# A mixture of experts on one core: the rows beyond 128 of a large expert in fp32 on four column tiles, and one chain of expert pairs

## The chip, the cores and the metric

The kernel runs on one core of a Trainium2 chip. The metric is the device time of one execution in microseconds. The core has TensorE (PE, with its weight loads shown apart as PEld), VectorE (DVE), ScalarE (ACT), GpSimd (POOL) and SyncE (SP), which issues most transfers. Engines run side by side and wait for each other through semaphores.

## The reference, cut to what matters

Two transformer blocks run one after the other on 512 rows of width 1024. The second one ends in a mixture of 32 experts, each row going to 4 of them:

```python
logits = (xf @ w_router + b_router).astype(jnp.float32)
top_v, top_i = lax.top_k(logits, TOP_K)
w = jax.nn.softmax(top_v, axis=-1)
...
h = lax.ragged_dot(xs, w_up, sizes) + b_up[sorted_e]
g, lin = jnp.split(h, 2, axis=-1)
g = jnp.minimum(g, SWIGLU_LIMIT)
lin = jnp.clip(lin, -SWIGLU_LIMIT, SWIGLU_LIMIT)
act = g * jax.nn.sigmoid(SWIGLU_ALPHA * g) * (lin + 1.0)
y = lax.ragged_dot(act, w_down, sizes) + b_down[sorted_e]
y = y * w.reshape(-1)[order][:, None].astype(y.dtype)
return jax.ops.segment_sum(y, tok, num_segments=n).reshape(B, T, D)
```

An expert has 1024 by 2048 and 1024 by 1024 fp32 weights, 12 MiB. Which rows it gets, and how many, is known only when the kernel runs.

## The kernel before, in words

The program is written out in order; a framework adds the semaphores. Everything up to the router is not touched by the change. In the experts' part (`moe`, from L1140) each expert's weights come as 12 chunks of 1 MiB, 8 for the up matrix and 4 for the down matrix, into a ring of 8 buffers of 128x2048. SP issues a chunk's transfer (`fetch`, L1120 in the trace) once the buffer's old content has been used (`refill`, L1131).

There are three ways to compute an expert:

- **`expert(e, two)`** (L1424), up to 128 rows. Each chunk is split into a high and a low fp32r part (`split`, L214: ACT copies, DVE subtracts), two chunks ahead, and its buffer is refilled right after. A step (`part`, L1323) is 4 k by 3 matmuls of 512 columns: x high by w high, x high by w low, x low by w high.
- **`few(e)`** (L1511), up to 64 rows, in fp32 straight from the ring (`halves`, L1488): two column tiles of 64 side by side, each a half of the columns, 8 matmuls of 256 columns a step. The buffer is refilled after its matmuls.
- **the second tile**, rows 128 to 191 of an expert, inside `expert` when `two` is 64 (`second`, L1444). It uses the split weights, two steps behind the first tile. Its 64 rows stand beside their low parts, so that a step is 8 matmuls of 512 columns and `sums` (L1438) adds the halves of the result.

The numbers of rows per expert are sorted on the chip (`order`, L1725), and `places` (L1208) branches on them: expert 0 first, in the form that its count asks for (`kind`); then, if any expert has still more rows, a loop (`far`) that loads its weights once more; then the pairs of a large expert (odd numbers) and a small one (even numbers). `seconds` (L1235) is a nest of up to 6 pairs with a second tile, left when t0, the number of experts with over 128 rows, is reached. Six single branches and `pairs` (L1241) take the other large ones, up to nP pairs; `rest` takes the small ones in between and `few(31)` is last.

What one expert prepares for the next stands in `ahead` (L1549): the row numbers of four experts at a time (`slots`, in step 6 of every expert with e % 4 == 1), the gather of the rows of expert e + 2 on POOL's queue in step 2, and their transposes (`flip`, L1311), which share two PSUM buffers (`tr`) with `slots`. `further` (L1564) does the same for the second tile. `finish` (L1366) weights an expert's result and scatters it with an add into the output rows on POOL's queue; a large expert's result is finished in step 0 of the small one that follows. The result tile `y` is also where `few` keeps its activations for the down matrix (`hf`, copied at L1541).

The order of the second tile and the first in `expert`:

```python
for i in range(12):
    n = e * 12 + i
    if two and i > 1:
        second(i - 2)
    if i < 10 or not e:
        self.unfold(n + 2)
    if i < 2:
        self.refill(n)
    self.part(self.bank(e, i), x if i < 8 else m["h"], i, self.pairs[n % self.PAIRS], one)
```

Of the kernel before, what the change touches and what calls it, by code (L numbers as in the profile page):

```python
# [11 lines left out]
F32 = mybir.dt.float32  # L12
# [22 lines left out]
def constants():  # L35
    c = np.zeros((128, CSTW), np.float32)

    def put(name, a):
# [25 lines left out]
                                e > 0, 128 + 64 * (e == 0) + 128 * (p[:, None] // 32), e, np.zeros((128, 7))], 1))  # L64
# [23 lines left out]
def lay_out(inp):  # L88
# [27 lines left out]
    for j in range(4):  # L116
# [19 lines left out]
        a["w_up_2"][0][..., q.ravel()].reshape(NE, 2, 4, 128, 4, 512).transpose(0, 4, 1, 3, 2, 5)).reshape(NE, 8, 128, 2048)  # L136
    o["w_dn2"] = np.ascontiguousarray(
        a["w_down_2"][0].reshape(NE, 2, 4, 128, 2, 512).transpose(0, 4, 1, 3, 2, 5)).reshape(NE, 4, 128, 2048)
# [17 lines left out]
class K:  # L156
# [983 lines left out]
    def moe(self):  # L1140
        tc, nc, a = self.tc, self.nc, self.a
        with ExitStack() as es:
# [26 lines left out]
            m["one64"] = mp.tile([128, 2, 128], F32R, name="one64")  # L1169
            nc.vector.memset(m["one64"].bitcast(F32), 0.0)  # L1170
# [35 lines left out]
    SECOND = 6  # L1206

    def places(self, srt):  # L1208
# [6 lines left out]
        kind = load(0, 2)  # L1215
        with tc.If(kind > 0) as cmp:
            with tc.If(kind < 2) as cm2:
                self.expert(0, 0)
            with cm2.Else():
                self.expert(0, 64)  # L1220
        with cmp.Else():
            self.few(0)
        nfar, nP, t0 = load(7, 64), load(1, 15), load(2, self.SECOND)
        with tc.If(nfar > 0):
            self.extra(srt)
            with tc.For_i(0, nfar, 1) as it:
                er = nc.values_load(self.li[0:1, ds(it, 1)], engines=(mybir.EngineType.SP, mybir.EngineType.DVE),
                                    min_val=0, max_val=NE - 1, skip_runtime_bounds_check_because="an expert's number")
                self.far(er, it)
# [5 lines left out]
        def seconds(t):  # L1235
            if t < self.SECOND:
                with tc.If(t0 > t):
                    pair(t, 64)
                    seconds(t + 1)
# [18 lines left out]
        seconds(0)  # L1258
        for lo in range(0, self.SECOND, 3):
            with tc.If(t0 < lo + 3):  # L1260
                for t in range(lo, lo + 3):
                    with tc.If(t0 < t + 1):
                        with tc.If(nP > t):
                            pair(t, 0)
        pairs(self.SECOND)
# [73 lines left out]
    def swiglu(self, i, bank, act, rows=128):  # L1339

        nc, m = self.nc, self.m
        j = i // 2
        if i not in (3, 5, 7):
            return
        n = 512 if j == 1 else 256
        pg, pl = (bank(0), bank(2)) if j == 1 else (bank(i - 1)[:, :256], bank(i - 1)[:, 256:])
        self.gated(pg, pl, act[:rows, 512 * (j > 1) + 256 * (j > 2):][:, :n])

    def gated(self, pg, pl, act):
        nc, m = self.nc, self.m  # L1350
        rows, n = act.shape
        sg = m["sg"][:rows, :n]
        nc.scalar.activation(sg, pg, AF.Relu, scale=-1.0, bias=m["seven"][:rows, 0:1])  # L1353
# [70 lines left out]
    def expert(self, e, two):  # L1424
        nc, m = self.nc, self.m
        one = m["one"][e % 2]
        x = m["x"][e % 2]
        sb = m["sl"][2]
        bb = m["bb"]
        self.numbers(e)  # L1430
        if two and not e:
            self.further(e)
        if two == 64:
            nc.vector.tensor_copy(m["one64"][:, :, :64], one[:, :, :64])
        xt = m["xb"][0]
        xb, tmp = ((xt[:, :, :64], xt[:, :, 64:]), m["y"][0][:64]) if two == 64 else (m["xb"], None)

        def sums(p, to):  # L1438

            nc.scalar.activation(to, p[64:], AF.Copy)  # L1440
            nc.vector.tensor_tensor(to, to, p[:64], op=OP.add)
            return to

        def second(i):  # L1444
            if i == 8:
                self.flip(m["actb"][0], xb, n=two)
            bank = lambda i: bb[i // 2 % 2] if i < 8 else bb[i % 2]
            self.part(bank(i), xt if two == 64 else xb, i, self.pairs[(e * 12 + i) % self.PAIRS],
                      m["one64"] if two == 64 else one, two)
            if two == 64 and i in (3, 5, 7):  # L1450
                h = [sums(bank(j), tmp[:, 512 * (j // 2 % 2):][:, :512]) for j in ((0, 2) if i == 3 else (i,))]
                self.swiglu(i, lambda j: h[min(j // 2, len(h) - 1)], m["actb"][0], 64)
            elif two == 128:
                self.swiglu(i, bank, m["actb"][0])

        for i in range(12):
            n = e * 12 + i
            if two and i > 1:
                second(i - 2)
            if i < 10 or not e:  # L1460
                self.unfold(n + 2)
            if i < 2:
# [466 lines left out]
```

## Time and profile before

| | us |
|---|---|
| median of 3 runs (2643.07 to 2645.09) | 2645.02 |
| time of the profiled execution | 2647.34 |
| its span | 2645.5 |
| busy in the span: PE | 2437.4 (92%) |
| PEld | 1948.2 (74%) |
| DVE | 1345.4 (51%) |
| ACT | 1062.9 (40%) |
| POOL | 191.7 (7%) |

The span is from the first to the last instruction; the time of an execution also has what lies around it. The experts' first matmul with weights (L1330) starts at 1335.9 us. Before that the two blocks' attention and dense layers run, and behind the experts a short tail. PE's busy time counts matmuls that overlap in the pipeline, so that a stretch with a busy PE need not run at its highest rate; the starts of instructions tell more. The mean granted TensorE clock is 0.966 of the full 2.4 GHz. A large expert can be told in the timeline by its first bias matmul (L1330, 512 columns), a small one by L1505 and L1509 (256 columns), and a second tile by its PSUM tile `pv`.

### The profile page before, as it was taken

The numbers are of one execution on the slowest core, as the hardware profiler recorded it, in microseconds if no ns is written. First come the engines' busy times: TensorE is split into PE (matmuls) and PEld (weight loads), VectorE is DVE, ScalarE is ACT, GpSimd is POOL, SyncE is SP. The second block draws the span as 40 slices with busy tenths as digits, with TensorE's granted clock in tenths as the row PEclk, the third lists the DMA queues.
The fourth block names the chain that finished last, engine by engine and source line by source line (L and its number), as shares of the span: only waits on it lengthen the run. The fifth ranks groups of instructions, "written<-read, shape, count | busy, mean of one in ns | idle before, by whom it ended". The sixth has DMA issues, their size and how long they took to land. (4 is left out here: it accounts for less than half of the span.)

```text
span 2645.5 us, 39434 instructions
## 1 busy us (share of the span) xinstructions
PE 2437.4 (92%) x15686; PEld 1948.2 (74%) x15686; DVE 1345.4 (51%) x2493; ACT 1062.9 (40%) x1596; POOL 191.7 (7%) x183
## 2 busy tenths in 40 slices
PE   7999999999999999999879899799999999688888
PEld 5799978898899899889857667476666666444457
DVE  6766753344333444467576536465656565121135
ACT  5755552223322325566354434344444444111123
POOL 0021100000000000000010100111100111000000
PEclk9999999999999999999989999899999999899999
DMA  4122222322222311210585966899999999899991
GB/s 157 64 94 71 77 72 96 124 92 80 96 96 87 121 54 65 83 60 2 186 291 195 350 248 237 303 374 366 404 376 402 366 402 377 297 400 399 400 380 41
DMA packets 86919, 554.54 MB, mean 210 GB/s; under 512 B 11783, under 2 KB 12935, under 8 KB 25368
## 3 DMA queue, kind: packets, MB, share of 16 engines
q1 hardware_dynamic: 71280, 508.33, 49.3%
q0 software_dynamic: 8784, 31.59, 4.7%
q10 hardware_dynamic: 6616, 11.53, 1.3%
q8 instruction: 138, 2.26, 0.4%
q14 instruction: 101, 0.83, 0.1%
HBM read 531.60 MB, written 19.81 MB: 208 GB/s over the span
## 5 line engine op out<-in xcount | busy, mean ns | idle before, releaser
L243 PE MATMUL mm<-b,wh 128*128 128x512 f32 (+1 forms) x1840 | 512.4, 365 | 1.7 <-ACT b L220 0.8
L243 PEld LDWEIGHTS mm<-b,wh 128*128 128x128 f32 x1840 | 328.7, 190 | 65.0 <-issue 3.4
L243 PE MATMUL mm<-b,wl 128*128 128x512 f32 (+2 forms) x920 | 335.2, 365 | 1.3 <-DVE wl L203 1.3
L243 PE MATMUL mm<-wh,b 128*128 128x256 f32 x1488 | 284.4, 288 | 1.5 <-DVE b L673 0.8
L203 DVE TENSOR_TENSOR wl<-raw,wh 128x2048 fp32r<-128x2048 f32 x81 | 185.5, 2290 | 176.5 <-ACT wh L202 176.4
L202 ACT ACTIVATE wh<-raw 128x2048 fp32r<-128x2048 f32 x81 | 155.1, 1915 | 260.9 <-PE mm L243 248.6
L243 PEld LDWEIGHTS mm<-wh,b 128*128 128x128 f32 x1488 | 236.0, 191 | 4.6 <-DVE b L673 1.2
L243 PE MATMUL mm<-wl,b 128*128 128x256 f32 x744 | 213.2, 287 | 1.0 <-DVE wl L203 1.0
L218 DVE TENSOR_TENSOR wl<-b,wh 128x2048 fp32r<-128x2048 f32 x76 | 173.5, 2289 | 55.0 <-ACT wh L217 54.8
L243 PEld LDWEIGHTS mm<-b,wl 128*128 128x128 f32 (+1 forms) x920 | 174.4, 190 | 31.6 <-DVE wl L203 2.2
L217 ACT ACTIVATE wh<-b 128x2048 fp32r<-128x2048 f32 x76 | 145.4, 1914 | 94.1 <-DMA b<-w_dn 38.3
L1509 PE MATMUL lg<-b,xf 128*64 128x256 f32 x1280 | 154.3, 386 | 16.4 <-DMA b<-w_up 9.3
L243 PEld LDWEIGHTS mm<-wl,b 128*128 128x128 f32 x744 | 142.2, 191 | 2.5 <-DVE wl L203 1.3
L1509 PEld LDWEIGHTS lg<-b,xf 128*64 128x64 f32 x1280 | 94.4, 139 | 66.9 <-DMA b<-w_up 15.0
L211 POOL TENSOR_TENSOR rs<-rm,c_nhalf 128x1 f32<-128x1 f32 (+3 forms) x52 | 52.9, 1019 | 1162.9 <-DVE rm L209 1154.6
L1353 ACT ACTIVATE sg<-lg,seven 128x128 f32<-128x128 f32 (+2 forms) x48 | 21.7, 452 | 232.5 <-PE lg L1509 179.5
L1509 PE MATMUL mm<-b,xf 128*64 128x256 f32 x640 | 78.8, 385 | 8.3 <-DMA b<-w_up 8.1
L1509 PE MATMUL mm<-pp,xf 128*64 128x256 f32 x640 | 79.0, 384 | 6.7 <-DMA pp<-w_up 6.6
L1541 DVE COPY b<-tr 128x128 f32<-128x128 f32 (+1 forms) x60 | 20.0, 334 | 124.0 <-PE tr L1540 90.1
L1355 DVE SCALAR_TENSOR_TENSOR sg<-mm,sg 128x256 f32<-128x256 f32 (+2 forms) x48 | 19.2, 399 | 124.4 <-ACT sg L1354 124.4
L1509 PE MATMUL mm<-b,b 128*64 128x256 f32 x480 | 63.3, 410 | 20.6 <-DVE b L1541 20.0
L1509 PEld LDWEIGHTS mm<-b,xf 128*64 128x64 f32 x640 | 46.6, 138 | 36.0 <-DMA b<-w_up 13.6
(541 smaller groups left out, 4825.1 us busy)
## 6 DMA issues: line engine op xcount, KB each, us to landing
b<-w_up SPq DMA_DIRECT2D x190, 1024.0 KB, 14.4
b<-w_dn SPq DMA_DIRECT2D x96, 1024.0 KB, 9.9
pp<-w_up SPq DMA_DIRECT2D x64, 1024.0 KB, 14.9
raw<-w_in SPq DMA_DIRECT2D x39, 1024.0 KB, 4.8
pp<-w_dn SPq DMA_DIRECT2D x32, 1024.0 KB, 9.9
raw<-w_up SPq DMA_DIRECT2D x16, 1024.0 KB, 5.1
raw<-w_down SPq DMA_DIRECT2D x16, 1024.0 KB, 4.8
raw<-w_out SPq DMA_DIRECT2D x8, 1024.0 KB, 4.8
```

What stands on the lines that cost most here:

```text
L202: nc.scalar.activation(wh, raw, AF.Copy)
L203: nc.vector.tensor_tensor(wl, raw, wh.bitcast(F32), op=OP.subtract)
L211: self.nc.gpsimd.tensor_tensor(r, m, self.c["nhalf"][:, :n], op=OP.pow)
L217: nc.scalar.activation(hi, src, AF.Copy)
L218: nc.vector.tensor_tensor(lo, src, hi.bitcast(F32), op=OP.subtract)
L243: self.nc.tensor.matmul(ps, l, r, start=(i == 0), stop=(i == n - 1))
L1353: nc.scalar.activation(sg, pg, AF.Relu, scale=-1.0, bias=m["seven"][:rows, 0:1])
L1355: nc.vector.scalar_tensor_tensor(sg, pg, 7.0, sg, op0=OP.min, op1=OP.mult)
L1509: nc.tensor.matmul(o[n], x(4 * kh + k), cut(w[:, k], n), start=not up and kh == k == 0, stop=kh == 1 and k == 3)
L1541: nc.vector.tensor_copy(hf[:, t0:t1].rearrange("p t a r -> p t (a r)"), p[:, :t1 - t0])
```

## The change

Four things change.

1. The second tile has 32 rows (128 to 159) and is computed in fp32 straight from the ring: four column tiles of 32 side by side, each a quarter of the 512 columns, 16 matmuls of 128 columns a step. It runs one step ahead of the first tile in the place of two behind, and a buffer of the ring is refilled after it (`second` returns, then `refill`). No fp32r parts, no sums. The bias comes in the same form, 4 matmuls per pair of up steps. The columns of the down matrix are reordered on the host so that the four tiles' activations can be transposed in two blocks of 128.
2. In a pair the small expert (odd number) comes first and the large one (even number) second. A large expert is finished at its own end.
3. `seconds`, the six single branches and `pairs` become one nest `pairs`. Its first 4 pairs (`SECOND`) always run the second tile, whatever the count.
4. The rare cases (expert 0 with at most 64 rows, or any expert with more rows than its tiles hold) stand in the else of one branch on `plain`. The sort puts the experts at other places and needs fewer counts.

The diff, cut to its core:

```diff
@@ places
-    SECOND = 6
+    SECOND = 4
-        kind = load(0, 2)
-        with tc.If(kind > 0) as cmp:
-            with tc.If(kind < 2) as cm2:
-                self.expert(0, 0)
-            with cm2.Else():
-                self.expert(0, 64)
-        with cmp.Else():
-            self.few(0)
-        nfar, nP, t0 = load(7, 64), load(1, 15), load(2, self.SECOND)
-        with tc.If(nfar > 0):
+        plain = load(2, 1)
+        with tc.If(plain > 0) as cmp:
+            self.expert(0)
+        with cmp.Else():
+            kind, nfar = load(0, 1), load(7, 64)
...
+        nP = load(1, 15)
-        def pair(t, two):
-            self.expert(1 + 2 * t, two)
-            self.few(2 + 2 * t, True, two and t + 1 < self.SECOND)
...
         def pairs(t):
             if t < NE // 2 - 1:
                 with tc.If(nP > t):
-                    pair(t, 0)
+                    self.few(1 + 2 * t, True, t < self.SECOND)
+                    self.expert(2 + 2 * t, t < self.SECOND)
                     pairs(t + 1)
...
-        seconds(0)
-        for lo in range(0, self.SECOND, 3):
...
-        pairs(self.SECOND)
+        pairs(0)
@@ expert
         for i in range(12):
             n = e * 12 + i
...
+            if i < 10:
+                self.split(*self.pairs[(n + 2) % self.PAIRS], self.raw(n + 2))
+                if not two:
+                    self.refill(n + 2)
...
-            self.part(self.bank(e, i), x if i < 8 else m["h"], i, self.pairs[n % self.PAIRS], one)
-            if i == 0 and e > 1:
+            self.part(bank(i), x if i < 8 else m["h"], i, self.pairs[n % self.PAIRS], one)
+            if two:
+                for k in range(i + (i > 0), min(i + 2, 12)):
+                    self.second(k, e)
+                    self.refill(e * 12 + k)
+            if i == 0 and e:
                 self.finish(e - 1, False)
...
         if two:
+            self.second_finish()
+        self.finish(e, True)
...
+    def second(self, i, e):
...
+        act, hf = [m["y"][0][:, 256 * a:256 * a + 256] for a in range(2)]
...
+        o = [p[32 * g:32 * g + 32, :128] for g in range(4)]
...
+        w = self.raw(e * 12 + i).rearrange("p (k f) -> p k f", k=4)
+        for k in range(4):
+            kk = 4 * kh + k
+            x = m["xs"][:, kk] if up else hf[:, kk // 4, kk % 4]
+            for g in range(4):
+                nc.tensor.matmul(o[g], x, self.cut(w[:, k], up, j, g, 4), start=not up and kh == k == 0, stop=kh == 1 and k == 3)
...
+        if i in (5, 7):
+            t = i // 6
+            q = self.tr()[:, 0]
+            nc.tensor.transpose(q, act[:, 128 * t:128 * t + 128], self.ident)
+            nc.vector.tensor_copy(hf[:, t].rearrange("p g r -> p (g r)"), q)
...
+    def second_finish(self):
...
+        for c in range(2):
+            for g in range(4):
...
+        self.scatter(m["actb"][0], m["sl"][2], 0, 32)
@@ further
-        self.gather(m["actb"][0], m["sl"][2], 0)
+        self.gather(m["actb"][0], m["sl"][2], 0, 32)
```

What the program issues, at the places that matter. On PE, inside a large expert with a second tile, before (`pv` is the second tile's PSUM tile, `lg` and `mm` are the first's):

```order
L1336 MATMUL lg<-b_12224,b_12232 128x512 x12
L1330 MATMUL pv<-bup,one_12241 128x512
L1336 MATMUL pv<-raw,xb 128x512 x8
L1330 MATMUL mm<-bup,one_12238 128x512
L1336 MATMUL mm<-wh,b_12232 128x512
L1336 MATMUL mm<-wl,b_12232 128x512
```

and in the change, where the weights of the second tile are the ring's buffers themselves (`pp`, `b`) and its rows are `xs`:

```order
L1322 MATMUL mm<-raw,b_12232 128x512 x12
L1482 MATMUL pv<-pp,xs 32x128 x16
L1322 MATMUL mm<-b_12224,b_12232 128x512 x12
L1476 MATMUL pv<-bup,one_12237 32x128 x4
L1482 MATMUL pv<-b_12225,xs 32x128 x16
L1316 MATMUL lg<-bup,one_12237 128x512
```

A second-tile step was 8 matmuls of 512 columns and is 16 of 128 columns that write 32 rows each. It stands between two steps of the first tile, as before.

On POOL's queue, one pair with a second tile, before (`b` with `acc` is a scatter, `xs` a gather; `s2i` are the second tile's row numbers):

```order
L1307 DMA acc<-b_12234,s0i 640x1024
L1303 DMA xg<-xs,s1i 64x1024
L1307 DMA acc<-b_12234,s2i 640x1024
L1307 DMA acc<-b_12234,s0i 640x1024
L1303 DMA b_12234<-xs,s2i 128x1024
L1237 COMPARE_AND_BRANCH
L1303 DMA b_12234<-xs,s1i 128x1024
L1307 DMA acc<-b_12234,s1i 640x1024
```

and in the change:

```order
L1235 COMPARE_AND_BRANCH
L1289 DMA b_12234<-xs,s1i 64x1024
L1289 DMA b_12234<-xs,s2i 32x1024
L1289 DMA xg<-xs,s0i 128x1024
L1293 DMA acc<-b_12234,s1i 640x1024
L1293 DMA acc<-b_12234,s2i 640x1024
L1293 DMA acc<-b_12234,s1i 640x1024
L1235 COMPARE_AND_BRANCH
```

The scatters of the second tile and of the large expert still follow each other, now both ahead of the pair's branch; the gather of the second tile has 32 rows and comes before them.

On PE behind the nest of pairs with a second tile, before; the trace comes here after its third pair:

```order
L1509 MATMUL mm<-pp,b_12234 64x256 x16
L1237 UNCONDITIONAL_BRANCH x7
L1213 TENSOR_LOAD ovi
L1260 COMPARE_AND_BRANCH
L1262 COMPARE_AND_BRANCH
L1263 COMPARE_AND_BRANCH
L1330 MATMUL lg<-bup,one_12238 128x512
```

and in the change at the end of a pair with a second tile, where the next pair follows in the same nest:

```order
L1482 MATMUL pv<-pp,b_12234 32x128 x16
L1303 MATMUL tr<-c_ident,b_12234 128x128 x2
L1322 MATMUL mm<-raw,h 128x512 x12
L1482 MATMUL pv<-pp,b_12234 32x128 x16
L1322 MATMUL mm<-b_12224,h 128x512 x12
L1235 COMPARE_AND_BRANCH
L1517 MATMUL lg<-bup,one_12238 64x256 x2
L1521 MATMUL lg<-b_12225,xf 64x256 x16
```

The row of branches, the load of a count and three more branches have gone, and the last step of the second tile stands ahead of the last of the first tile.

## Rows read from the trace of the kernel before

**Rows 1.** Timeline, TensorE: start us, duration, instruction, idle before; starts of large experts
```profile
1388.29 0.78 PE L1330 MATMUL lg<-bup,one 128*128 128x512 f32 x1 [11.13 <-PEq L1224]
...
1487.91 0.50 PE L1330 MATMUL lg<-bup,one 128*128 128x512 f32 x1
...
1586.03 0.50 PE L1330 MATMUL lg<-bup,one 128*128 128x512 f32 x1
...
1699.79 0.76 PE L1330 MATMUL lg<-bup,one 128*128 128x512 f32 x1 [12.04 <-DVEq L1260]
...
1764.03 0.50 PE L1330 MATMUL lg<-bup,one 128*128 128x512 f32 x1
...
1836.49 0.50 PE L1330 MATMUL lg<-bup,one 128*128 128x512 f32 x1
...
1902.21 0.50 PE L1330 MATMUL lg<-bup,one 128*128 128x512 f32 x1
...
2268.84 1.12 PE L1505 MATMUL lg<-bup,one 128*64 128x256 f32 x4 [18.63 <-DVEq L1250]
```

**Rows 2.** Windows: PE, PEld, DVE, ACT, POOL busy, granted clock, DMA share, GB/s
```profile
1467.00:1488.00 21.00, 14.18 (x111) 8.45 (x108) 6.79 (x15) 7.22 (x8) 3.02 (x3) 0.84 1.02 391
1530.00:1555.00 25.00, 25.00 (x121) 18.12 (x121) 10.64 (x17) 10.04 (x17) 0.00 (x0) 1.00 0.36 127
```

**Rows 3.** Timeline, TensorE: a second-tile step, and the end of that large expert
```profile
1506.00 2.03 PE L1336 MATMUL pv<-raw,xb 128*128 128x512 f32 x8
...
1507.86 0.39 PE L1330 MATMUL mm<-bup,one 128*128 128x512 f32 x1
...
1515.57 0.60 PE L1317 MATMUL tr<-c_ident,b 128*128 128x128 f32 x4
...
1515.93 0.48 PE L1330 MATMUL pv<-bup,one 128*128 128x512 f32 x1
...
1553.01 3.45 PE L1509 MATMUL mm<-b,xf 128*64 128x256 f32 x29
```

**Rows 4.** Timeline, TensorE: a small expert without waits
```profile
1739.21 0.65 PE L1505 MATMUL mm<-bup,one 128*64 128x256 f32 x4
...
1739.70 3.62 PE L1509 MATMUL mm<-b,xf 128*64 128x256 f32 x32
...
1757.15 0.66 PE L1317 MATMUL tr<-c_ident,b 128*128 128x128 f32 x4
...
1757.65 0.27 PE L1540 MATMUL tr<-c_ident,b 128*128 128x128 f32 x1
...
1757.85 1.95 PE L1509 MATMUL mm<-b,b 128*64 128x256 f32 x16
```

**Rows 5.** Groups by line and shape: an fp32 matmul on the whole array (busy, mean ns)
```profile
L575 PE MATMUL lg<-xc,w_rg 128*128 128x512 f32 x32 | 15.4, 604 | 0.4 <-DVE xc L571 0.4
```

**Rows 6.** Timeline, TensorE: eight bf16 matmuls with a weight load each
```profile
1344.24 0.35 PE L1829 MATMUL tr<-rwt,oh 128*128 128x6 bf16 x8
1344.45 0.48 PE L1330 MATMUL mm<-bup,one 128*128 128x512 f32 x1
```

**Rows 7.** Timeline, POOL and TensorE: two scatters, and the wait of a small expert
```profile
1555.54 1.42 POOL L1307 DMA_INDIRECT acc<-b,s2i  x1 [26.96 <-ACT b L1481]
...
1563.66 1.57 POOL L1307 DMA_INDIRECT acc<-b,s0i  x1 [6.70 <-DVE s2i L1836]
...
1575.11 3.68 PE L1509 MATMUL mm<-b,b 128*64 128x256 f32 x16 [5.92 <-DVE b L1541]
```

**Rows 8.** Branch instructions of one line on PE's queue: duration ns, start
```profile
L1224 PEldq COMPARE_BRANCH  x1: 6431/6431/6431, 1381.1 to 1381.1; - x1
```

**Rows 9.** Timeline, TensorE, and window: slots inside a large expert
```profile
1786.28 0.35 PE L1829 MATMUL tr<-rwt,oh 128*128 128x6 bf16 x8
...
1791.00 0.51 PE L1317 MATMUL tr<-c_ident,xg 64*128 64x64 f32 x4 [3.34 <-DVE h L218]
...
1790.00:1800.00 10.00, 9.00 (x31) 5.91 (x32) 7.86 (x20) 6.38 (x5) 0.00 (x0) 0.56 1.02 424
```

More of the change, by code (lines that the diff above doesn't have):

```diff
@@ L1422, in last, with expert @@
             self.split(self.y[0][:64, cc], self.y[1][:64, cc], y)
-    def expert(self, e, two):
+    def expert(self, e, two=False):
         nc, m = self.nc, self.m
[L1426 to L1429, printed above, removed]
+        one, x, act = m["one"][e % 2], m["x"][e % 2], m["act"][0]
+        bank = partial(self.bank, e)
         self.numbers(e)
[L1431 to L1454, printed above, removed]
@@ L1475, in expert @@
         if two:
-            second(10)
-            second(11)
-            y = m["actb"][0][:two]
-            for c in range(2):
-                p = sums(bb[c], tmp[:, 512 * c:512 * c + 512]) if two == 64 else bb[c]
-                nc.scalar.activation(y[:, 512 * c:512 * c + 512], p, AF.Copy, scale=sb["w"][:two, 0:1])
-            self.scatter(m["actb"][0], sb, 0, two)
-        if not e:
-            if two:
-                self.further(e + 1)
-            self.finish(e, True)
+            self.second_finish()
@@ new lines, in expert, with cut, second_rows @@
+        self.finish(e, True)
+    def cut(self, w, up, j, n, of):
+        if up and j > 1:
+            return w.rearrange("p (a b f) -> p a b f", a=2, b=of)[:, :, n]
+        return w[:, 512 // of * n:512 // of * (n + 1)]
+    def second_rows(self):
+        nc, m = self.nc, self.m
+        for k in range(0, KC, 4):
+            p = self.tr()[:, :, :32]
+            for i in range(4):
+                nc.tensor.transpose(p[:, i], m["actb"][0][:32, (k + i) * 128:(k + i + 1) * 128], self.ident[:32, :32])
+            nc.vector.tensor_copy(m["xs"][:, k:k + 4], p)
@@ new lines, in second_finish @@
+    def second_finish(self):
+        nc, m = self.nc, self.m
+        y, w = m["actb"][0][:32], m["sl"][2]["w"][:32, 0:1]
+        for c in range(2):
+            for g in range(4):
+                p, o = m["bb"][c][32 * g:32 * g + 32, :128], y[:, 512 * c + 128 * g:][:, :128]
+                if g % 2:
+                    nc.vector.tensor_scalar(o, p, w, None, op0=OP.mult)
+                else:
+                    nc.scalar.activation(o, p, AF.Copy, scale=w)
+        self.scatter(m["actb"][0], m["sl"][2], 0, 32)
@@ L1524, in few @@
                 self.unfold(n + 2)
-            if i == 0 and e > 1:
-                self.finish(e - 1, paired)
+            if i == 0 and e and e % 2 == 0:
+                self.finish(e - 1, False)
             self.ahead(e, i, 8, paired)
-            if i == 3 and (second or not e):
+            if i == 3 and second:
                 self.further(e + 1)
@@ L1543, in few @@
                 self.last_rows(e)
[L1544 removed]
+        if e % 2 == 0:
             self.finish(e, False)
@@ L1556, in ahead @@
             if f < NE:
-                self.gather(m["xg"][f % 2], m["sl"][f // 4 % 2], f % 4, 128 if f % 2 and (at == 6 or not e) else 64)
+                self.gather(m["xg"][f % 2], m["sl"][f // 4 % 2], f % 4, 64 if f % 2 or at == 8 and e else 128)
         if i == 2 and e + 1 < NE:
@@ L1561, in ahead @@
             f, k = (e + 1) % 2, 4 * (i - at)
-            self.flip(m["xg"][f], m["x"][f] if both else None, k, k + 4, n=128 if both else 64, whole=m["xf"])
+            self.flip(m["xg"][f], m["x"][f] if both else None, k, k + 4, n=128 if both else 64, whole=None if both else m["xf"])
     def further(self, e):
```

119 lines of the change are left out of this document (60 added, 59 removed).

## The prediction

> **What bounds the kernel now.** I read the TensorE timeline first, for the starts of the large experts [rows 1]. Until the first expert with 512 wide matmuls nothing is touched by the change, so only the chain of pairs counts: it runs from 1377.2 us (1388.29 less the gap of 11.13) to 2250.2 (2268.84 less 18.63), 873.0 us. In it a start to start distance is one large expert and one small one. Two distances with a second tile are 99.6 and 98.1 us; the third is 101.7 plus a gap of 12.04. Without a second tile the first pair takes 64.2, then 72.5 and 65.7 in turn; the seven from 1764.03 to 2250.2 have a mean of 69.5.
>
> The windows say which resource sets these [rows 2]. In a large expert with a second tile PE is busy throughout while the DMA share is 0.36: TensorE is the bound, the ring of eight weight buffers is full and SP waits. In the small expert the share is 1.02 at 391 GB/s: the ring is being refilled. So what TensorE does less in such a pair comes off the end. A plain pair is nearly level: 24 chunks of 1 MiB are 25.2 MB, at 391 GB/s 64 us, and its PE work is little less.
>
> **The change, part by part.** The large expert with a second tile runs 65.1 us, from 1487.91 to 1553.01 [rows 1, 3]. Its second tile is 12 steps of 8 matmuls of 512 columns; eight take 1.86 us (1506.00 to 1507.86), 233 ns each, so 96 of them 22.4. With four bias matmuls (0.9), 16 transposes of 64 rows (1.3) and a start wait of 1.0 it is 25.6 us; 39.5 stay for the first tile and what lies between.
>
> The new second tile does 12 steps of 4 k by 4 column tiles, 192 fp32 matmuls of 128 columns, and 16 for the bias. Each fp32 matmul stands in the trace as two records, so 416 records. No row shows four column tiles of 32. The nearest row is the small expert, two column tiles of 64, same data type and same moving matrix: 32 records in 3.62 us, 113 ns for 256 columns [rows 4]. One fp32 record of 512 columns on the whole array costs 481 ns (15.4 us by 32) [rows 5], 240 for 256, so two tiles overlap all but fully. The same for four tiles of 128 columns is a quarter of 113, 28 ns. That is the floor, and the order of what PE can take at all: eight tiny bf16 matmuls with their weight loads go in 0.21 us, 26 ns a pair [rows 6]. The top is no overlap, 481 by 4, 120 ns. I take 33, a little over the floor that the same form of work reaches, since that floor and the tiny matmuls' 26 ns meet: 416 by 33 is 13.7 us.
>
> The Trainium skill ("TensorE: Matmul & The Clock Gate", Part 3, measured speedup) gives 2.38 for three column tiles, 79% of ideal; an estimate by that page is 120/4/0.79 or 38 ns for four, and the sum below would be 8 us longer. No run here shows it yet.
>
> Going from one tile shape to another costs time too: between two small steps five transposes take 0.70 us (1757.15 to 1757.85) [rows 4], and four in a row without a change take 0.36 (1515.57 to 1515.93), 0.09 each, so 0.25 is left for two changes. The 12 steps need 24 changes: 3.1 us. Ten transposes add 0.9. I add 0.5 for the transpose in step 7 that needs the activations of that step. Second tile: 18.2 us, in place of 25.6, and the large expert 57.7.
>
> The small expert costs 24.8 us where nothing holds it (1739.21 to 1764.03) but 33.0 in this stage (1553.01 to 1586.03). PE waits 5.92 us there for a copy into the tile that the scatter of the large expert still reads, and its next 16 records then take 3.68 us, twice the usual [rows 7]. The wait hangs on two scatters into the same rows, one behind the other: the second tile's at 1555.54, the first tile's at 1563.66, 8.1 us later; the wait ends at 1575.11, 11 us on. In the change both still follow each other, but the second tile's last step now stands ahead of the first tile's last one on PE, so its scatter can go some 4 us earlier against the small expert's start. I leave 2.5 us of the wait, with 0 and 5.9 as ends: 27.3 us. On POOL only the next gathers queue behind the waiting scatter; they are wanted a whole expert later. A pair with a second tile is 57.7 + 27.3 = 85.0 us.
>
> There are **four** such pairs now, not three: the count is fixed at four, while the trace runs three before it leaves that branch. The fourth pair pays for a tile that holds no rows.
>
> Jumps: a taken branch, as the one over the loop for rare cases, costs 6.4 us on PE's queue [rows 8]. The 12.04 us gap at 1687.75, out of the first chain and past three pairs, is gone with the single chain. Between the first expert and the chain two long jumps became one, so that gap falls from 11.1 to 4.7. The 18.63 behind the chain stays: the jumps to the rest are the same three. Dropped count arithmetic ahead of the chain is a few DVE operations, under 1 us; I count nothing. In the second-tile experts SP refills a buffer only after the fp32 step has read it, about a step later than after the split. The 0.36 share covers that; with a DMA-bound pair it would cost a chunk, 2.7 us.
>
> Plain pairs: the 72.5 against 65.7 us have a cause in the trace. Every fourth expert number (e%4 == 1) computes the slots of four experts, and today these are large experts. There the eight slot matmuls take one of the two transpose buffers; the row gather's transposes then wait 3.34 us for the other, and the granted clock of the ten microseconds around is 0.56, mostly its lower level of 1.2 GHz [rows 9]. With the small expert first, odd numbers are small, and the slots move into them, where hardly a split of weights stands in DVE's queue. I take 66 us for all of them, and 64.2 for the first, which finds a full ring.
>
> **Sum.** Gap 4.7, four pairs 340.0, one at 64.2, six at 66.0 (396.0): 804.9 us against 873.0, so 68 less. The profiled execution has a span of 2645.5 and a time of 2647.3; 2577 and 2579 are expected. It stands 2.3 us over the median of 2645.0, so the median should be **2577 us**.
>
> **The rivals.**
> *Only two column tiles at a time.* The rows show two and no more. A record then costs half of 113, 57 ns: 10 us a pair, 40 in all, 2617.
> *The plain pairs gain nothing.* The swap moves the slots but leaves DMA and TensorE level, and something else makes the slow pair. Against it: the alternation follows the slots exactly. For it: 24 chunks at 391 GB/s fill 64 us of a pair by themselves. Six pairs at 69.5 add 21: 2598.
> *Everything overlaps.* 28 ns a record (8 us less), no wait in the small expert (10 less), plain pairs at the 64.2 of the first (11 less): 2548.
> *Slower: the tiles do not overlap.* Each narrow matmul waits for the one ahead, at 120 ns: 416 by 87 more is 36 us a pair, 145 in all, 2722. It decides from 74 ns a record on, where 41 ns more by 416 by 4 eat the 68 us. The small expert speaks against it: its two tiles share all rows of the array, and a lack of overlap would show 240 ns instead of 113.
> The Trainium skill speaks for this rival: the same page, Part 3, says that a weight load overlaps with running matmuls only where the row group differs, and all four tiles here use the same rows. By that rule the loads would stand between the matmuls, and the time would be near this rival's; the two-tile row disagrees with it, so it gets a small chance.
> *The plain branch is not taken.* With over 160 rows in an expert, the rare branch adds two jumps and at least 12 MiB of unhidden weights, 13 + 32 us: 2622. The three pairs only show that three experts have over 128 rows; the reference's router on its inputs gives 149, 143 and 130, and 127 for expert 0.
>
> **How the numbers follow.** Chances: forecast 0.50, plain pairs without gain 0.18, everything overlaps 0.14, two tiles at a time 0.12, slower 0.05, rare branch 0.01. Ends of the unknown costs: 28 to 57 ns is -8 to +40 us, the wait -10 to +14. The range of 2548 to 2618 reaches from the best case to two tiles at a time and leaves out the slower rival and the worse combinations. 0.2% is 5.3 us, about what a measurement of this kernel tells from no change. Slower by that needs over 74 ns a record: 0.05; within it 0.02; faster 0.93.
>
> **What would show it.** Right: four starts of large experts some 85 us apart, 32 of the narrow records in about 1.1 us, no gap of 12 us in the chain, plain pairs without alternation near 66, a wait for the copy of 0 to 3 us. Wrong: narrow records over 50 ns apart; second pairs over 95 us; plain pairs still at 72 and 66; a small expert of 33 us, which would mean that the scatters still hold it.

## The result, and the profile after

The changed kernel takes **2603.97 us** (median of 4 runs, 2600.15 to 2604.55) against 2644.05 us of the kernel before in the same session: a ratio of 0.985, 95% interval 0.9832 to 0.9868, 40 us less. The forecast was 2577 in a range of 2548 to 2618: right in sign and in range, with 27 us of the gain missing.

The head of the page of the kernel after, and its line of engines:

```profile
span 2598.1 us, 41846 instructions
PE 2425.4 (93%) x17042; PEld 1941.2 (75%) x17042; DVE 1326.2 (51%) x2473; ACT 1043.5 (40%) x1578; POOL 174.5 (7%) x184
```

The profiled execution's own time is 2600.15 us, and its span is 47.4 us under the 2645.5 of before. That is 7 us more than the medians differ by, because the profiled run of before lies 3.3 us above its median and this one 3.8 us below its own. TensorE's timeline of the kernel after has the starts of the small experts; each now opens a pair (columns: start, duration, engine, line, operation; in brackets the idle time before and what ended it):

```profile
1385.37 0.65 PE L1517 MATMUL lg<-bup,one 128*64 128x256 f32 x4
...
1467.41 0.65 PE L1517 MATMUL lg<-bup,one 128*64 128x256 f32 x4
...
1637.33 0.65 PE L1517 MATMUL lg<-bup,one 128*64 128x256 f32 x4
...
1721.18 0.65 PE L1517 MATMUL lg<-bup,one 128*64 128x256 f32 x4
...
1864.06 0.65 PE L1517 MATMUL lg<-bup,one 128*64 128x256 f32 x4
...
1934.82 0.65 PE L1517 MATMUL lg<-bup,one 128*64 128x256 f32 x4
...
2003.26 0.65 PE L1517 MATMUL lg<-bup,one 128*64 128x256 f32 x4
...
2142.23 0.65 PE L1517 MATMUL lg<-bup,one 128*64 128x256 f32 x4
...
2226.92 1.12 PE L1517 MATMUL lg<-bup,one 128*64 128x256 f32 x4 [12.12 <-DVE one L1286]
```

From 1385.37 to 1721.18 are the four pairs with a second tile: 335.8 us, 84.0 each, where three took 98 to 102 before [rows 1]. From 1721.18 to 2214.80 (2226.92 less the gap of 12.12) are seven plain pairs: 493.6 us, 70.5 each. There the forecast had 460.2. The alternation shrank to 70.8 and 68.4 (the pairs from 1864.06 and from 1934.82), but its mean did not fall.

One step of the new second tile, also from TensorE's timeline, answers to [rows 3] and [rows 4]:

```profile
1424.12 1.08 PE L1482 MATMUL pv<-pp,xs 128*32 128x128 f32 x32
1425.13 3.07 PE L1322 MATMUL mm<-raw,b 128*128 128x512 f32 x12
```

32 records from 1424.12 to 1425.13 are 31.6 ns each, at a granted clock of 1.00: set against the 120 ns that the prediction worked out for no overlap, four column tiles run almost wholly at the same time.

What TensorE waited for through the chain, first after, then before (columns: who waited, for whom, total us, times, longest):

```profile
PE mm L1322 <- DVE wl L220: 30.0, 18, 2.4
PE tr L1459 <- DVE b L220: 7.7, 2, 4.1
```

```profile
PE mm L1509 <- DVE b L1541: 20.0, 3, 7.3
PE tr L1317 <- DVE h L218: 16.8, 7, 3.3
PE lg L1330 <- DVEq L1260: 12.0, 1, 12.0
PE lg L1330 <- PEq L1224: 11.1, 1, 11.1
...
PE lg L1336 <- DVE wl L218: 3.5, 7, 0.7
```

The waits that the change set out to remove are gone: the copy held by the scatter (20.0), the transposes behind the slots (16.8), both jump gaps (12.0, 11.1). In their place stands, above all, a wait that was 3.5 us and is now **30.0**: large-expert matmuls for the low half `wl` that VectorE's subtraction writes. The 7.7 us are a new wait at the start of the second tile. Over the whole chain TensorE's idle time fell from 71.6 to 43.8 us and its busy time from 801.5 to 785.6.

### The profile page after: what moved, and what is told of

It reads as the page before. It is cut to its first block, busy times and chain, and to the rows that moved or that the text cites. A ratio compares the mean times of both kernels' runs of the same rounds, so it can differ in the third digit from the quotient of the medians.

```text
span 2598.1 us, 41846 instructions
## 1 busy us (share of the span) xinstructions
PE 2425.4 (93%) x17042; PEld 1941.2 (75%) x17042; DVE 1326.2 (51%) x2473; ACT 1043.5 (40%) x1578; POOL 174.5 (7%) x184
## 5 line engine op out<-in xcount | busy, mean ns | idle before, releaser
L245 PEld LDWEIGHTS mm<-b,wh 128*128 128x128 f32 x1840 | 328.8, 190 | 65.4 <-issue 3.4
L205 DVE TENSOR_TENSOR wl<-raw,wh 128x2048 fp32r<-128x2048 f32 x81 | 185.5, 2290 | 176.2 <-ACT wh L204 176.2
L220 DVE TENSOR_TENSOR wl<-b,wh 128x2048 fp32r<-128x2048 f32 x74 | 169.2, 2288 | 65.4 <-ACT wh L219 62.4
L1521 PE MATMUL lg<-b,b 128*64 128x256 f32 x1024 | 130.7, 394 | 7.5 <-DMA b<-w_dn 7.2
L1521 PEld LDWEIGHTS lg<-b,b 128*64 128x64 f32 x1024 | 76.0, 141 | 49.1 <-issue 11.5
L1345 ACT ACTIVATE sg<-mm,seven 128x128 f32<-128x128 f32 (+2 forms) x48 | 21.8, 455 | 223.2 <-PE mm L1521 180.9
L1521 PE MATMUL mm<-pp,xf 128*64 128x256 f32 x640 | 84.3, 388 | 4.6 <-DMA pp<-w_up 4.5
L1347 DVE SCALAR_TENSOR_TENSOR sg<-lg,sg 128x256 f32<-128x256 f32 (+1 forms) x48 | 19.2, 399 | 127.6 <-ACT sg L1346 127.6
L1345 ACT ACTIVATE sg<-lg,seven 128x256 f32<-128x256 f32 (+1 forms) x48 | 21.7, 452 | 146.1 <-PE lg L1521 118.4
```

The costliest lines, as they stand in the source:

```text
L205: nc.vector.tensor_tensor(wl, raw, wh.bitcast(F32), op=OP.subtract)
L220: nc.vector.tensor_tensor(lo, src, hi.bitcast(F32), op=OP.subtract)
L245: self.nc.tensor.matmul(ps, l, r, start=(i == 0), stop=(i == n - 1))
L1347: nc.vector.scalar_tensor_tensor(sg, pg, 7.0, sg, op0=OP.min, op1=OP.mult)
L1521: nc.tensor.matmul(o[n], x(4 * kh + k), cut(w[:, k], n), start=not up and kh == k == 0, stop=kh == 1 and k == 3)
```

## The experiments

All times are medians of 4 or 5 runs, each group beside runs of the kernel before (2644 to 2646 us). Since the first expert's length moves by some 8 us from kernel to kernel (last section), plain pairs are compared by the trace: the mean of four, from the start of small expert 13 to that of 21 (12 to 20 where the large expert comes first). Such a mean is from one run of the kernel, and runs of one kernel can differ by more than 10 us: three second tiles took 2575.4 to 2588.9 us, of which the trace has the fastest, and of half of each load it has the slowest (2601.8).

| run | time, us | ratio to before (95%) | plain pair, us |
|---|---|---|---|
| before | 2644 to 2646 | 1 | 69.2 |
| the change | 2604.0 | 0.985 (0.9832 to 0.9868) | 69.5 |
| three second tiles | 2583.8 | 0.9768 (0.974 to 0.9797) | 69.8 |
| half of each load | 2594.0 | 0.9798 (0.9773 to 0.9824) | 70.1 |
| half of each subtraction | 2584.9 | 0.9763 (0.9732 to 0.9795) | 67.9 |
| before, slots moved | 2628.5 | 0.9933 (0.9908 to 0.9959) | 66.9 |
| tile by tile | 2663.3 | 1.0073 (1.0056 to 1.009) | 69.7 |
| three tiles, border | 2590.6 | 0.9796 (0.978 to 0.9813) | 70.6 |
| three tiles, GpSimd helps | 2595.6 | 0.9819 (0.9801 to 0.9837) | 72.5 |
| three tiles, later gather | 2580.0 | 0.9748 (0.9725 to 0.9771) | 70.3 |
| three tiles, copy ahead | 2573.3 | 0.972 (0.9702 to 0.9738) | 68.7 |
| three tiles, splits in order | 2566.4 | 0.970 (0.9681 to 0.9719) | 67.5 |
| the same, later gather | 2564.3 | 0.9692 (0.9664 to 0.9719) | 67.9 |
| the same, half of each load | 2526.0 | 0.9546 (0.953 to 0.9562) | 63.9 |

**The tile of no rows.**

```
-    SECOND = 4
+    SECOND = 3
```

> The changed kernel with three second tiles in place of four; the fourth large expert holds 126 rows, so its tile was empty. If a second tile costs what the four distances of 82.0 to 86.4 us against 70.5 us of a plain pair say, the time falls by 13 to 20 us, to about 2588 (the fourth pair then takes 64 to 72 us). Rival: the empty tile is hidden under the weight stream and the time stays within 4 us of 2604.

20 us less. By the trace the fourth pair takes 69.3 us in place of 83.9, 14.6 less; the chain also starts 5.0 us earlier, because the first expert, which the edit does not touch, itself begins that much earlier (1334.33 in place of 1339.38). The fourth pair of the change, with no rows in its second tile, took 83.9 us, and the three with rows 82.0 to 86.4: an empty second tile costs what a full one does.

**Are the column tiles what makes it fast?** The same matmuls, but four of one column tile in a row:

```
-        for k in range(4):
-            kk = 4 * kh + k
-            x = m["xs"][:, kk] if up else hf[:, kk // 4, kk % 4]
-            for g in range(4):
+        for g in range(4):
+            for k in range(4):
+                kk = 4 * kh + k
+                x = m["xs"][:, kk] if up else hf[:, kk // 4, kk % 4]
                 nc.tensor.matmul(o[g], x, self.cut(w[:, k], up, j, g, 4), start=not up and kh == k == 0, stop=kh == 1 and k == 3)
```

> The changed kernel with one edit in the second tile: all four k of one column tile in a row, then the next column tile, so that neighbouring matmuls use the same column tile. Theory, the 32 ns a record come from neighbours on different column tiles running at the same time: a record then takes up to the 120 ns of no overlap, 416 records by up to 88 ns are up to 37 us a pair, 146 us in all, time 2650 to 2750. Rival, 32 ns is what TensorE needs to take in a record of this size whatever tile it goes to: no change, 2600 to 2610.

TensorE's timeline of this run, at the same step:

```profile
1424.43 2.46 PE L1482 MATMUL pv<-pp,xs 128*32 128x128 f32 x32
1426.82 1.41 PE L1322 MATMUL mm<-b,b 128*128 128x512 f32 x5
```

32 records now take 2.39 us (1424.43 to 1426.82), 75 ns each; the four pairs take 99.4 us each (the first starts at 1378.08, the fifth at 1775.85) in place of 84.0, and the kernel is slower than before, 2663 us. Weight loads are as many in both runs (PEld x17042), and the granted clock is 1.00 at both steps. So without the alternation of the tiles the second pairs take what they took before the change (98.1 to 101.7 us). 75 ns are less than the 120 that the prediction had for no overlap; whether neighbours on one tile overlap in part or the 120 was too high was not tried.

**Three suspects for the plain pair**: the weight stream, VectorE's subtractions, the slots.

```
-        (queue or self.nc.sync).dma_start(self.raw(n), src)
+        w = 1024 if 108 <= n < 276 else 2048
+        (queue or self.nc.sync).dma_start(self.raw(n)[:, :w], src[:, :w])
```

> Leaves out half of each weight chunk's load in the plain pairs (experts 9 to 22), nothing else. Theory A, the weight stream sets the plain pair: the mean of 70.5 us falls to what TensorE needs by itself, 61.7 to 64 us, seven pairs 45 to 60 us less, time 2545 to 2560. Theory B, VectorE's subtractions in the large expert set it: only the wait of the first split for its chunk goes (3.6 us on ScalarE, 1.6 on TensorE), a pair stays at 67 to 69 us, time 2585 to 2595. Theory C, the gather and scatter set it: no change beyond 5 us.

This run computes with half of the weights missing. The pair takes 70.1 us, which is no theory's number, though the time of 2594.0 us lies in theory B's range. VectorE's timeline of this run, in one pair, shows why; TensorE's row for the end of it follows:

```profile
1955.66 4.49 DVE L220 TENSOR_TENSOR wl<-b,wh 128x2048 fp32r<-128x2048 f32 x2 [5.41 <-ACT wh L219]
1960.07 0.28 DVE L1348 SCALAR_TENSOR_TENSOR sg<-mm,sg 128x128 f32<-128x128 f32 x1
```

```profile
1961.41 0.47 PE L1551 MATMUL tr<-c_ident,b 128*128 128x128 f32 x1 [4.58 <-DVE b L1350]
```

The small expert's gate (L1348) stands behind two subtractions for the next large expert; TensorE, 4.58 us idle, waits for the gate. How the instructions of one engine follow each other is settled when the kernel is built, and it came out differently here. Leaving work out had changed the order too.

```
+            if w:
+                lo, src, hi = [t[:, :w] for t in (lo, src, hi)]
             nc.vector.tensor_tensor(lo, src, hi.bitcast(F32), op=OP.subtract)
...
+                self.split(*self.pairs[(n + 2) % self.PAIRS], self.raw(n + 2), w=1024 if 108 <= n < 276 else None)
```

> Leaves out half of each subtraction on VectorE (1024 of 2048 columns, 2.29 us to about 1.15) in the plain pairs, nothing else. Theory A, the weight stream sets the plain pair: it falls at most to the 66 us at which the stream never pauses, time 2570 to 2600. Theory B, VectorE sets it: the waits of TensorE for the subtraction (58 us over six pairs) go and the pair falls to 62 to 64 us, time 2545 to 2560.

The pairs without slots fall to 65.4 us, those with slots stay at 70.5 (from 1995.18 to 2065.66). VectorE is busy for 12.1 us less a pair (115.9 in place of 164.2 us over the four), and that is worth 1.6 us: its sum of work is not the bound either. The 58 us that theory B counted on were too many: over the six pairs from 1721 us on, TensorE's matmuls of the change waited 24.5 us for `wl`.

```
-        if i == 1 and e == 0 or i == 6 and e % 4 == 1 and e + 3 < NE:
-            f = e // 4 * 4 + 4 if e else 0
+        if i == 1 and e == 0 or i == 6 and e % 4 == 0 and e + 4 < NE:
+            f = e + 4 if i == 6 else 0
```

> The kernel before with one edit: the slots of four experts are computed in a small expert (numbers 0, 4, 8 and so on) and no longer in a large one. Theory of the prediction, the slots in the large expert make the slow pair: no alternation, seven pairs near 66 us in place of a mean of 69.5, time 2645 less 15 to 25, about 2625. Rival, a slow pair only makes up what the fast one before it ran ahead, or DMA sets the mean: pairs still have a mean of 69 to 70 us, time within 5 us of 2645.

Start of small experts 12 and 20, from TensorE's timeline of this run:

```profile
1868.44 0.65 PE L1505 MATMUL mm<-bup,one 128*64 128x256 f32 x4
...
2136.19 0.65 PE L1505 MATMUL mm<-bup,one 128*64 128x256 f32 x4
```

267.75 us by four are 66.9, with no alternation beyond 1.2 us. So the prediction's theory of the slots was right, in the old order of the pair; its gain was there and the swap lost it again.

**What the swap did.** Timelines of the changed kernel in the slots pair that starts at 1864.06, first ScalarE and VectorE, then TensorE:

```profile
1886.93 1.91 ACT L219 ACTIVATE wh<-b 128x2048 fp32r<-128x2048 f32 x1 [1.88 <-DMA b<-w_up]
...
1888.88 2.29 DVE L220 TENSOR_TENSOR wl<-b,wh 128x2048 fp32r<-128x2048 f32 x1 [3.10 <-ACT wh L219]
1891.09 0.68 DVE L220 TENSOR_TENSOR b<-tr,b 128x512 fp32r<-128x512 f32 x1
1891.69 0.28 DVE L1551 COPY b<-tr 128x128 f32<-128x128 f32 x1
```

```profile
1891.22 0.50 PE L1322 MATMUL mm<-wl,b 128*128 128x512 f32 x1 [1.60 <-DVE wl L220]
...
1892.59 2.81 PE L1521 MATMUL lg<-b,b 128*64 128x256 f32 x24
```

The small expert's last 24 records need the copy at 1891.69. It stands behind a subtraction for the next large expert, which itself waited 3.10 us for ScalarE's copy, as that had waited for its chunk to land. Meanwhile TensorE begins that large expert, and waits 1.60. And in the large expert of the next pair:

```profile
1984.97 2.29 DVE L220 TENSOR_TENSOR raw<-pp,raw 128x2048 fp32r<-128x2048 f32 x1 [0.80 <-ACT raw L219]
...
1987.51 2.28 DVE L220 TENSOR_TENSOR wl<-b,wh 128x2048 fp32r<-128x2048 f32 x1
...
1990.84 2.29 DVE L220 TENSOR_TENSOR b<-pp,b 128x2048 fp32r<-128x2048 f32 x1
1993.04 2.29 DVE L220 TENSOR_TENSOR wl<-b,wh 128x2048 fp32r<-128x2048 f32 x1
```

```profile
1989.85 0.50 PE L1322 MATMUL mm<-wl,h 128*128 128x512 f32 x1 [2.35 <-DVE wl L220]
1993.36 0.72 PE L1322 MATMUL mm<-raw,h 128*128 128x512 f32 x2
1995.39 0.51 PE L1322 MATMUL mm<-wl,h 128*128 128x512 f32 x1 [1.30 <-DVE wl L220]
```

Chunk 10 (`raw`) is split ahead of chunk 8 (`wl`), chunk 11 (`b`) ahead of chunk 9 (`wl`), while TensorE wants 8 and 9 first: one split of 2.29 us too early, 2.35 us of wait; again, 1.30. Three guesses at what to do about it, on the kernel with three second tiles, were misses:

```
                     self.few(1 + 2 * t, True, t < self.SECOND)
-                    self.expert(2 + 2 * t, t < self.SECOND)
+                    with tc.If(nP > t):
+                        self.expert(2 + 2 * t, t < self.SECOND)
```

> Three second tiles, and a block border between the small expert and the large one behind it, so that no first matmul of the large expert stands ahead of the small expert's last 24 records on TensorE's queue. Theory, the swap lost the plain pairs' gain there (TensorE waits 1.6 to 2 us for the first split with small-expert work queued behind it, and everything after starts later): plain pairs fall from 68.4 and 70.6 to 66 to 68 us, time 10 to 25 us under the 2584 of three second tiles. Rival, VectorE's subtractions set the pair wherever TensorE's queue is cut: within 5 us of 2584.

70.6 us: the border only moves the wait from the large expert into the small one, where the same copy keeps TensorE idle for 4.23 us:

```profile
1888.93 5.18 PE L1522 MATMUL lg<-b,b 128*64 128x256 f32 x24 [4.23 <-DVE b L1552]
```

That is the miss that named the cause: not TensorE's queue but the copy's place in VectorE's.

```
+            if share:
+                c = slice(2048 - share, 2048)
+                nc.gpsimd.tensor_tensor(lo[:, c], src[:, c], hi[:, c].bitcast(F32), op=OP.subtract)
+                lo, src, hi = [t[:, :2048 - share] for t in (lo, src, hi)]
             nc.vector.tensor_tensor(lo, src, hi.bitcast(F32), op=OP.subtract)
...
+                self.split(*self.pairs[(n + 2) % self.PAIRS], self.raw(n + 2), share=512 if e and not two and 2 < i else 0)
```

> Three second tiles, and in the plain large experts GpSimd does 512 of the 2048 columns of the subtraction from the sixth chunk on. Theory, VectorE sets the large expert: its part falls from 2.29 to about 1.7 us, seven of twelve splits, 4 us less of VectorE a pair, pairs 1 to 3 us shorter, time 2565 to 2580. Rivals: GpSimd's part takes longer than VectorE's whole (over 2.3 us for 512 columns) or slows VectorE: time over 2590.

Groups of this run, one of GpSimd's over the span and two of VectorE's over the plain pairs (after the count: busy us, mean ns of one):

```profile
L222 POOL TENSOR_TENSOR wl<-b,wh 128x512 fp32r<-128x512 f32 x24 | 55.6, 2317 | 42.2 <-ACT wh L219 33.1 <-PE mm L1326 9.1
```

```profile
L224 DVE TENSOR_TENSOR wl<-b,wh 128x1536 fp32r<-128x1536 f32 x18 | 42.2, 2344 | 0.0
L224 DVE TENSOR_TENSOR wl<-b,wh 128x2048 fp32r<-128x2048 f32 x18 | 41.2, 2290 | 25.5 <-ACT wh L219 22.5 <-issue 2.6
```

VectorE takes 2344 ns for 1536 columns beside GpSimd and 2290 for 2048 alone, where three quarters of that would be 1718. Nothing is gained and the pairs take 72.5 us. The Trainium skill says why it might be so ("SBUF — State Buffer", section "SBUF: two separate sides"): a VectorE operation with two SBUF inputs and a GpSimd operation lock each other out of a shared port. These rows agree with it, but no run has GpSimd's part by itself.

```
-        for f in [e + 2] * (i == 2) + [1] * (i == 1 and e == 0):
+        for f in [e + 2] * (i == (7 if e % 2 and e > 6 else 2)) + [1] * (i == 1 and e == 0):
```

> Three second tiles, and in the small experts of the plain pairs the gather for the next small expert is put five steps later, so that it no longer runs right behind the large expert's scatter, where the transfer rate falls to 83 GB/s for 3 us. Theory, this dip makes the first chunk of the large expert late (it lands 20 us after the ring starts again, five chunks at 2.6 us would be 13): the first split comes 2 to 4 us earlier, pairs 1.5 to 3 us shorter, time 2564 to 2574. Rival, the dip is the scatter's, or the chunk is not what the pair waits for: within 5 us of 2584.

No change within the spread (2580.0 against 2583.8; pairs 70.3 against 69.8).

**The order put back.** First only the copy: the first two splits of the next large expert (`unfold`) are kept behind it on ScalarE and VectorE.

```
+                copied = nc.vector.tensor_copy(hf[:, t0:t1].rearrange("p t a r -> p t (a r)"), p[:, :t1 - t0])
...
+            if i > 9 and paired and e > 2 * self.SECOND:
+                with tc.issue_after(self.behind[0]), tc.issue_after(copied.ins):
+                    self.unfold(n + 2)
...
```

> Three second tiles, and in the plain pairs' small expert the first two weight splits of the next large expert are kept behind its last transposes' copies on ScalarE and VectorE (the order the kernel before had by itself). Theory O, VectorE's order of work made the plain pairs slow: in every second pair (the one with slots) the copy that the last 24 records of the small expert need stands behind a subtraction that waits for its chunk; that pair falls by 2 to 4 us from 70.5, the others stay at 68.4, eight pairs with four of that kind, time 8 to 16 us under the 2584 of three second tiles. Rival, the chunk arrives late and holds TensorE either way: within 5 us of 2584.

The pairs with slots fall from 70.8 to 68.5 us (1844.79 to 1913.31, and the others alike), those without stay at 68.9: 68.7 in the mean, and 10.5 us less in time, as theory O had it. Then the splits of the large expert too, each kept behind the one before on ScalarE and VectorE:

```
-                self.split(*self.pairs[(n + 2) % self.PAIRS], self.raw(n + 2))
+                with ExitStack() as es:
+                    if e and not two:
+                        for ins in last:
+                            es.enter_context(self.tc.issue_after(ins))
+                    self.split(*self.pairs[(n + 2) % self.PAIRS], self.raw(n + 2))
+                last = self.behind
```

> As the run before, and in the plain large experts the twelve splits are kept in the order in which TensorE uses them on ScalarE and VectorE; the changed kernel has chunk 10 ahead of chunk 8 and chunk 11 ahead of chunk 9. Theory O: TensorE's waits of 2.2 to 2.4 and 1.3 us in the large expert's down projection go, each of the eight plain pairs falls by 2 to 4 us more, to 65 to 67 us, time 2545 to 2565. Rival, VectorE's sum of work sets the large expert (36 us from its first split to its last) whatever the order: pairs stay at 68 us and more, time over 2570.

```profile
1836.00 0.65 PE L1525 MATMUL lg<-bup,one 128*64 128x256 f32 x4
...
2106.13 0.65 PE L1525 MATMUL lg<-bup,one 128*64 128x256 f32 x4
```

270.13 us by four are 67.5, and the time is 2566.4 us: 17 under three second tiles alone, and 38 under the change. That is 2.2 us a pair less than with the order as built (69.8). This second step gave 1.2 of them (68.7 to 67.5) where theory O had 2 to 4, and both figures lie just outside its ranges: of the two waits that were to go, the one of 1.30 went, and one of 2.29 stayed. With the next run, level with it, this is the fastest version that computes the reference. The same with the later gather:

> The three second tiles and the ordered splits of the last run, and the small experts' gather five steps later, away from the scatter. With the order in place the transfers never pause (share 1.0 in nearly all windows), so theory A: the weight stream is now the bound, and a dip less of 1 to 2 us a pair shows: 4 to 15 us under 2566. Rival, the gather moves the same bytes at another time and slows the chunks there as much: within 4 us of 2566.

2564.3, no difference that can be told, pairs 67.9: when the gather runs does not matter. And the loads halved once more, now with the splits held in order (half of the weights are missing here too):

> The three second tiles and the ordered splits, and half of each weight chunk of the plain pairs left out of the loads. Theory A, with the order in place the weight stream holds the pair: from a mean of 67.7 us it falls to 63 to 65 us, time 2530 to 2550. Rival B, VectorE's subtractions hold it (their sum in a large expert is 27.5 us of 2.29 each, some 38 us with the rest of VectorE's work): pairs stay at 66.5 us or more, time over 2555.

The windows of two plain pairs of this run, and of two of the run with full loads (columns: stretch, its length, then busy us of PE, PEld, DVE, ACT and POOL with counts, granted clock, DMA share, GB/s):

```profile
1828.96:1893.69 64.73, 63.73 (x401) 45.27 (x401) 41.19 (x58) 32.09 (x33) 11.19 (x4) 1.00 0.70 220
1893.69:1956.68 62.99, 62.00 (x386) 44.71 (x385) 40.22 (x52) 32.09 (x33) 11.19 (x4) 1.00 0.73 226
```

```profile
1836.00:1903.77 67.77, 65.46 (x401) 46.23 (x400) 41.69 (x58) 32.70 (x33) 4.99 (x4) 0.97 1.01 397
1903.77:1972.11 68.34, 64.52 (x386) 45.48 (x385) 40.61 (x52) 32.84 (x33) 6.30 (x4) 0.98 1.01 395
```

With half the bytes TensorE is busy for all but 1 us of a pair: 63.0 us without slots and 64.7 with them are its own work. With all bytes the DMA share is 1.01 throughout, and a pair takes 3.7 us more in the mean. About half of the difference between these windows is TensorE's own busy time, at a granted clock of 0.97 and 0.98 in place of 1.00.

The two runs differ in more than the bytes, though. The splits are held in order among themselves, but not against VectorE's other work. With full loads a copy of the next small expert's rows (`xf`) stands ahead of the split of chunk 8 and itself waits for TensorE's transposes; then TensorE waits for that split (VectorE's rows, then TensorE's):

```profile
1819.91 0.42 DVE L1308 COPY xf<-tr 128x256 f32<-128x256 f32 x1 [2.96 <-PE tr L1304]
1820.25 2.28 DVE L220 TENSOR_TENSOR wl<-b,wh 128x2048 fp32r<-128x2048 f32 x1
```

```profile
1822.59 0.50 PE L1323 MATMUL mm<-wl,h 128*128 128x512 f32 x1 [2.29 <-DVE wl L220]
```

This wait of 2.29 us comes once in each of the eight plain pairs. With half the loads the same copy came out behind the split, and TensorE has no wait for `wl` in the plain pairs:

```profile
1874.82 2.28 DVE L220 TENSOR_TENSOR wl<-b,wh 128x2048 fp32r<-128x2048 f32 x1
...
1878.61 0.41 DVE L1309 COPY xf<-tr 128x256 f32<-128x256 f32 x1
```

So the order of splits held the changed kernel's plain pair (69.8 to 67.5 us), and what was left is the weight stream and this copy together (67.5 to 63.9). How much of it is the copy was not tried. For the stream as the larger part speaks that no run with full loads has a mean under 66.9, that of the old order with its slots moved, where the DMA share is 1.02. Halving the stream alone, with the order as it came, gave nothing (70.1).

## Why the prediction was right, and where it failed

- **The record.** 33 ns forecast from the two-tile row and the tiny matmuls, 31.6 measured. Set against 120 ns that is 3.8 times, and against the 75 measured for four in a row on one tile 2.4 times. From the figure of the Trainium skill ("TensorE: Matmul & The Clock Gate", Part 3, measured speedup) for three column tiles the estimate was 38 ns; four came nearer to their ideal here. By the rule of the same page of the Trainium skill that a weight load overlaps with running matmuls only where the row group differs, the slower rival would have come; the trace disagrees, as weight loads are busy for 0.81 of the 1.01 us in which these matmuls never pause. *Only two column tiles* and *no overlap* fell.
- **The second pairs.** 85.0 forecast, 84.0 measured (335.8 in place of 340.0 for four). The wait for the copy behind the scatters, of which I left 2.5 us a pair, went wholly. The new tile has a start wait, for which its sum had no term (the 1.0 stands with the old tile): 7.7 us in two of the four.
- **The fourth pair.** Paid for an empty tile, as said: 14.6 us.
- **The jumps.** The 12.04 us gap is gone. The gap behind the first expert, left at 4.7, is gone too, but the first expert takes 46.0 us (1339.38 to 1385.37) in place of 41.3 and starts 3.5 later. The 18.63 at the chain's end, said to stay, is 12.12, and the rest behind it takes 5.5 us less (371.2 against 376.7): small gains that the prediction did not have, and whose cause was not tried.
- **The plain pairs: the step that failed.** "With the small expert first, odd numbers are small, and the slots move into them, where hardly a split of weights stands in DVE's queue. I take 66 us for all of them, and 64.2 for the first, which finds a full ring." Measured are 70.5 in the mean and 72.8 for the first; that is 33.4 us of the sum, more than the whole miss. Its first half was right: with the slots moved and nothing else, the old order gives 66.9. Its second half took over the fast pair's 66 us into another order of work without asking what stands where on VectorE, and its premise was wrong: splits do stand in DVE's queue there, the one at 1888.88 ahead of the copy that the small expert needs. It weighed what the swap moves, the slots, and not what it newly puts side by side: a small expert's last copies and the next large expert's first splits now share one stretch of the program, and were interleaved there. Of the 4.5 us a pair, the order of the splits is shown for 2.2; the rest was not taken apart. The rival *plain pairs gain nothing* gave 2598 and came nearest, though not for its reason: in the old order the slots did make the slow pair, and what holds the pair in the new order it named only as "something else".
- **Luck.** 2604 lies in the range because its upper end was set by *only two column tiles*, a case that did not come; and 8.9 us that the gap and the second pairs gave beyond the forecast hid a part of the 33.4.

The account from span to span: first expert +8.2 (3.5 later, 4.7 longer), chain 829.4 in place of 873.0 or -43.6, gap behind it -6.5, rest -5.5; sum -47.4. In the chain against its forecast of 804.9: gap -4.7, second pairs -4.2, plain pairs +33.4, which is the 24.5 too much.

Left open: how the 3.7 us between full and half loads part into the weight stream and the copy ahead of chunk 8; 0.6 us a pair between the ordered splits (67.5) and the large expert first (66.9); and the order was tried on three second tiles only, not on four.

## What to carry to other kernels

A duration taken from a favourable stretch carries over only with the order of work that made it: when a change swaps two neighbours, list what then stands ahead of what on each in-order engine, above all which instruction that waits for a transfer now stands in front of one that the busiest engine needs. Where two limits lie within 10% of each other (here the weight stream and the splits), taking one away alone can show little or nothing, and an edit that leaves work out can change the order as well: hold the order fixed, of copies as well as of splits, then halve, and compare the order in both traces. And a tile count fixed in the code is paid for whether its rows exist or not.

## What the runs showed of the hardware that was not expected

- Column tiles that alternate are faster: 31.6 ns a record when neighbours go to different tiles, 75 when the four matmuls of one tile follow each other.
- GpSimd beside VectorE gained nothing: 512 columns took it 2317 ns, and VectorE's 1536 beside it 2344, against 2290 for all 2048 alone.
- The first expert, which is the same in all kernels with the small expert first, started between 1334.3 and 1342.1 us there and took from 41.9 to 50.2. TensorE waits in it for a gather to land: 1.03 us in the run tile by tile, 3.59 in the change, 7.75 in the run with the copy ahead. Totals that differ by less than that say little there; distances of pairs in the trace do.
